# Wider products for the spatial-gate values, the HGRN values and the per-layer gate of a hybrid decoder layer

## The chip, the cores and the metric

The kernel runs on one core of one Trainium2 chip. A core has a matrix engine (TensorE, PE in the profile, with its weight loads as PEld), a vector engine (DVE), a scalar engine (ACT), GpSimd (POOL) and an engine that only issues transfers (SP). The metric is the time of one execution on the device in microseconds; lower is better.

## The reference, cut to what matters

One decoder layer (batch 1, 512 tokens, width 1024, float32) with four token mixers side by side, a gated MLP, a gated per-layer embedding and a final norm. Three products are touched by the change: `v` of the spatial gate, `i` of the HGRN mixer and the gate of the per-layer embedding.

```
proj = rmsnorm(x, norm_mix) @ w_in
xa, xb, xc, xd, g = split(proj)                       # pool, rwkv7, spatial gate, hgrn2, branch gates
u, v = split(gelu(xc))                                # 512 columns each
v = layernorm(v) * ln_w + ln_b;  branch_2 = u * (W_s v + b)
q, f, i = split(xd)                                   # 512 columns each; i: the values of the HGRN recurrence
...
x = x + sum_k(sigmoid(g_k) * (branch_k @ w_branch_k)) @ w_out
x = x + ffn(rmsnorm(x, norm_ffn))
x = x + (p @ ple_proj) * sigmoid(rmsnorm(x, norm_ple) @ ple_gate)      # 1024 columns
out = rmsnorm(x, norm_final)
```

## The kernel before

Every large product is made exactly enough in float32 by splitting both operands into a high and a low part: `mm3` issues three matrix products for each 128 rows of contraction, `hi x hi`, `hi x lo` and `lo x hi` (lines 119, 120 and 121, which is why each large product shows up under these three lines). A weight is loaded by `wload` in chunks of 512 KB on SP's queue, cast to its high part on ACT (line 77) and subtracted to its low part on DVE (line 78). Two buffers hold raw chunks and four each hold high and low parts.

Most products put the weights in the array and move the 512 tokens past them (`gemm`). Three stages want tokens on the partitions, and there `gemm_tok` puts 128 tokens in the array and moves the weight columns past them. For the spatial-gate values (`sg_v`), the HGRN values (`hgrn_v`) and the per-layer gate (`ple`) a weight block (`wcols`) has 256 columns and comes in two chunks of four contraction tiles; each of the four token tiles is taken through all eight contraction tiles, 24 products, into one PSUM buffer, and then evicted, before the next token tile begins. The projection of the embedding at the start (`ple_proj_out`) uses `gemm_tok` with 512 moving columns.

PSUM has two pools of four banks: `mm` (pool `pm`) for the large products, `sm` (pool `ps`) for transposes, norms, the recurrences and the heads. SBUF tiles come from rings; the ring `f` has seven buffers of 512 columns and holds, among others, the four value tiles of the spatial gate, GELU scratch (`gz`) and the branch gates (`gt`).

The work of the mixers is written out in the string `ORDER`. Each word names a part; an exclamation mark makes it urgent, so that the planner puts it ahead of the products that fill in. The planner lays down each engine's instructions in a fixed order when the kernel is built: by priority among those that it holds to be ready, by its own costs. The recurrence of RWKV (`chain.j.half`) issues small products in steps that wait for DVE, and large products stand between the steps. In `ORDER`, `hv.0`, `hv.1` are the two column blocks of `hgrn_v` and `sgv.0`, `sgv.1` those of `sg_v`.

The last stage is the per-layer gate: blocks 0 and 1 run over the four token tiles each; then, for each token tile, blocks 2 and 3 are followed by the final norm of that tile and its stores. The scale `r2` of the norm before the gate is made by `sums` once the first 24 products have been issued.

Of the kernel before, what the change touches and what calls it, by code (L numbers as in the profile page):

```python
# [13 lines left out]
ALU = mybir.AluOpType  # L14
AX = mybir.AxisListType

P = 128
T = 512
NT = T // P
D = 1024  # L20
KD = D // P
# [14 lines left out]
# emission order of the mixers' parts; "!" puts a part before the matrix products that fill in  # L36
# [3 lines left out]
!chain.1.0 !cols hv.1 !sgv.0 !w.3 sgv.1 !chain.1.1 prep.2 !fin.1 merge.0.2 !forms.2 !x.3.1 sgn !sgu.1 sgu.0  # L40
!gate.3.0 merge.2.1 inv.2 !chain.2.0 x.3.0 !merge.2.0 !prep.3 forms.3 !chain.2.1 !gate.3.3 merge.2.2 inv.3
hg.1 !fin.2 merge.2.3 gate.3.2 !hg.0 !chain.3.0 !chain.3.1 fin.3 !out hv.0 !head.0 !head.3 !head.2 ho.3
# [6 lines left out]
def hybrid_kernel(ctx, tc, x, p, norm_mix, w_in, pool_w, pool_scale, rwkv_mu, rwkv_w0, rwkv_w2, rwkv_a0,  # L49
# [25 lines left out]
    # ---------------------------------------------------------------- weights  # L75
# [8 lines left out]
    def rsqrt(r, var, scale, eps, eng=S):  # L84
        """r = (var * scale + eps) ** -0.5 of a few columns."""
        if eng is G:
            V.tensor_scalar(r, var, scale, eps, ALU.mult, ALU.add)
            G.tensor_tensor(r, r, epst[:, 3:4].broadcast_to(list(r.shape)), ALU.pow)
        else:
            S.activation(r, var, AF.Sqrt, scale=scale, bias=epst[:, (NORM_EPS, 64e-5, 1e-5).index(eps):][:, 0:1])  # L90
            V.reciprocal(r, r)
# [6 lines left out]
    def wload(src, a, b, name, early=True):  # L98
        """a k-tiles of b columns as exact sums hi + lo; returns k -> (hi, lo)."""
        g = max(1, 1024 // b)  # L100
        res = []
        with (tc.high_priority() if early else nullcontext()):
            for k0 in range(0, a, g):
                kn = min(g, a - k0)
                raw, hi, lo = (wp.tile([P, 1024], dt, tag=tg, name=f"{tg}_{name}{k0}", bufs=nb)
                               for tg, dt, nb in (("wr", F32, NWR), ("wh", F32R, NWS), ("wl", F32R, NWS)))
                raw, hi, lo = (t[:, :kn * b].rearrange("p (a b) -> p a b", a=kn) for t in (raw, hi, lo))
                nc.sync.dma_start(raw, src[:, k0:k0 + kn, :])
                with (nullcontext() if loaded else tc.high_priority()):
                    split(raw, hi, lo)  # L110
                loaded.append(name)
                res += [(hi[:, k, :], lo[:, k, :]) for k in range(kn)]
        return res

    def wcols(w, c0, name, early=True):
        return wload(w[:, c0:c0 + WB].rearrange("(k p) c -> p k c", p=P), KD, WB, name, early)
# [16 lines left out]
    # -------------------------------------------------------------- constants  # L133
# [27 lines left out]
    # ------------------------------------------------------------------ start  # L161
# [16 lines left out]
    # per-layer embedding's projection, which needs no x; kept in DRAM until the end  # L178
# [49 lines left out]
    def spread(r, name):  # L228
        """r[t] of each token, tokens along the free axis, on every partition."""
        pr = sm_ps(f"ps{name}")  # L230
        for t in range(NT):
            dg = sp.tile([P, P], F32, tag="dg", name=f"dg{name}{t}")
            V.tensor_scalar(dg, ident, r[:, t:t + 1], None, ALU.mult)
            PE.matmul(pr[:, t * P:(t + 1) * P], ones, dg, start=True, stop=True)
        return pr
# [49 lines left out]
    # hgrn lower bound: softmax over the depth axis, inclusive sum less the first  # L285
# [10 lines left out]
    # =============================================================== mixers  # L296
# [3 lines left out]
    def branch_out(k, i, src):  # L300
        """channel tile i of branch k, as hi + lo for the branch's projection."""
        hi = rg.tile([P, T], F32R, tag="bo", name=f"boh{k}_{i}", bufs=NBO)
        lo = rg.tile([P, T], F32R, tag="bo", name=f"bol{k}_{i}", bufs=NBO)
        split(src, hi, lo, V)
        bo.setdefault(k, [None] * 4)[i] = (hi, lo)
# [4 lines left out]
    # ------------------------------------------------------------------ rwkv  # L310
# [8 lines left out]
    # decay and rate weights, hi and lo parts stacked along the contraction: one pass takes both  # L319
# [39 lines left out]
    def c4(t):  # L359
        """a tile as (chunk, head, 64 columns)."""  # L360
        return t.rearrange("p (c h x) -> p c h x", c=HC, h=2)

    def head_sum(o, src, name):
        """sums over each head's channels, on all of them."""
        hi, lo = (rt(f"hs{i}{name}", F32R) for i in range(2))
        split(src, hi, lo, V)
        PE.matmul(o, blkr, hi, start=True, stop=False)
        PE.matmul(o, blkr, lo, start=False, stop=True)
# [24 lines left out]
    def rwkv_prep(j):  # L393
# [20 lines left out]
        # per chunk: decayed -kk to read the state, and decayed r  # L414
# [15 lines left out]
        # columns (B, K) of each chunk's tokens  # L430
# [5 lines left out]
        # the same decayed to the chunk's end  # L436
# [4 lines left out]
        # chunk decays, channels of both heads on the lower partitions  # L441
# [5 lines left out]
        # states (below) and values (above) of both heads  # L447
# [8 lines left out]
        # the second head's reads on the lower partitions; the upper ones take the inverses  # L456
# [5 lines left out]
    def rwkv_forms(j):  # L462
        ard, BK, BD = (rw[j].pop(n) if n != "ard" else rw[j][n] for n in ("ard", "BK", "BD"))
        # rows: tokens of (B, K); columns: their products with A and R (masked)
# [19 lines left out]
        # unit lower triangular inverses of the diagonal 32-blocks, transposed, one block per lane  # L484
# [6 lines left out]
    def rwkv_inverse(j):  # L491
# [20 lines left out]
        # inverses of the 64-blocks from those of the 32-blocks  # L512
# [14 lines left out]
        # the reads of the state take the place of the inverted products  # L527
# [6 lines left out]
    def rwkv_chain(j, half):  # L534
        ard, AR, BKe, M, TA, TT, dec = (rw[j][n] for n in ("ard", "AR", "BKe", "M", "TA", "TT", "dec"))
        # state chain over the chunks
# [41 lines left out]
    def rwkv_finish(j):  # L578
# [3 lines left out]
        # group norm over each head  # L582
# [31 lines left out]
    # ------------------------------------------------------------------ pool  # L614
# [34 lines left out]
    # ------------------------------------------------------------------- sgu  # L649
# [10 lines left out]
    def sg_prep():  # L660
# [8 lines left out]
        # bias over (channel, token): ln_b[c] * rowsum(w)[g, t] + b[g, t], as a product over two rows  # L669
# [16 lines left out]
    def sg_v(vb):  # L686
        vs = sgd["vs"]
        w = wcols(w_in, sg0 + W + vb * WB, f"sgv{vb}")
        for t in range(NT):
            pt = mm_ps(f"psv{vb}_{t}")[:, :WB]  # L690
            gemm_tok(pt, w, hT, t)
            gelu_to(vs[t][:, vb * WB:(vb + 1) * WB], pt, WB, f"v{vb}_{t}")
# [33 lines left out]
    # ------------------------------------------------------------------ hgrn  # L726
# [19 lines left out]
    def hgrn_v(ib):  # L746
        w = wcols(w_in, hc0 + 2 * W + ib * WB, f"hgi{ib}")
        for t in range(NT):
            pt = mm_ps(f"phi{ib}_{t}")[:, :WB]
            gemm_tok(pt, w, hT, t)  # L750
            S.copy(it[t][:, ib * WB:(ib + 1) * WB], pt)
# [110 lines left out]
    # ----------------------------------------------------------------- merge  # L862
# [45 lines left out]
    # ================================================================== ffn  # L908
# [10 lines left out]
    def sums(acc, name):  # L919
        """1 / rms of each token, from squares summed over the channel tiles, tokens on partitions."""  # L920
        pt = sm_ps(f"ps_{name}")
        for t in range(NT):
            PE.matmul(pt[:, 2 * t:2 * t + 2], acc[:, t * P:(t + 1) * P], ones[:, 0:2], start=True, stop=True)
        r = sp.tile([P, NT], F32, tag="rr4", name=f"r_{name}")
        rsqrt(r, pt[:, 0:2 * NT:2], 1.0 / D, NORM_EPS)
        return r
# [104 lines left out]
    # ============================================== per-layer embedding, output  # L1031
# [16 lines left out]
    wpg, r2 = {}, []  # L1048

    def ple(nb, t):  # L1050
        cs = slice((nb % 2) * WB, (nb % 2 + 1) * WB)
        po = mm_ps(f"ppg{nb}_{t}")[:, :WB]
        gemm_tok(po, wpg[nb], x2n, t)
        if not r2:
            r2.append(sums(acc2, "p"))
        sg = bt(f"sg{nb}_{t}")[:, :WB]
        S.activation(sg, po, AF.Sigmoid, scale=r2[0][:, t:t + 1])
        V.tensor_tensor(sg, sg, pp[t, nb // 2][:, cs], ALU.mult)
        xo = x3[t, nb // 2][:, cs]
        V.tensor_tensor(xo, xo, sg, ALU.add)  # L1060
        acc = ssf[:, t, nb:nb + 1]
        if t < NT - 1:
            S.activation(sg, xo, AF.Square, accum_out=acc)
        else:
            V.scalar_tensor_tensor(sg, xo, 1.0, xo, ALU.mult, ALU.mult, accum_out=acc)

    for nb in range(4):
        wpg[nb] = wcols(ple_gate, nb * WB, f"pg{nb}")
        if nb < 2:
            for t in range(NT):  # L1070
                ple(nb, t)
    for t in range(NT):
        ple(2, t)
        if t == NT - 1:
            xn = at("xn", F32)
            G.tensor_tensor(xn, x3[t, 0], nf[0], ALU.mult)
        ple(3, t)
# [40 lines left out]
```

## Time and profile before

| | |
|---|---|
| time, median of 3 runs | 1156.05 us (1155.33 to 1156.17) |
| profiled execution, span from first to last instruction | 1153.9 us |
| profiled execution, own time | not given apart from the span; the median of the runs is 2.15 us above it |
| TensorE busy in the span | 1134.2 us, 98% |
| DVE, ACT, POOL busy | 754.7, 457.0, 205.9 us |
| granted TensorE clock, mean | 0.999 of full |

The profile is of one execution. A product's busy time runs from its start until its result is out, and the next one starts before that; the distance between two starts is what a product takes of the engine. "L119" is line 119 of the kernel; "out<-in" are the program's names. A view says of each instruction or group which engine it is on, its line, its shape and its times; idle time of an engine carries the instruction that ended it.

### The profile page before, as it was taken

The numbers are of one execution on the slowest core, as the hardware profiler recorded it, in microseconds if no ns is written. First come the engines' busy times: TensorE is split into PE (matmuls) and PEld (weight loads), VectorE is DVE, ScalarE is ACT, GpSimd is POOL, SyncE is SP. The second block draws the span as 40 slices with busy tenths as digits, with TensorE's granted clock in tenths as the row PEclk, the third lists the DMA queues.
The fourth block names the chain that finished last, engine by engine and source line by source line (L and its number), as shares of the span: only waits on it lengthen the run. The fifth ranks groups of instructions, "written<-read, shape, count | busy, mean of one in ns | idle before, by whom it ended". The sixth has DMA issues, their size and how long they took to land.

```text
span 1153.9 us, 16004 instructions
## 1 busy us (share of the span) xinstructions
PE 1134.2 (98%) x6170; PEld 919.9 (80%) x6170; DVE 754.7 (65%) x1354; ACT 457.0 (40%) x675; POOL 205.9 (18%) x232
## 2 busy tenths in 40 slices
PE   7999999999999999999999999999999999999997
PEld 5777776887888777878777888888888888888897
DVE  5689986768795688556666565476766766333345
ACT  5733632445342423232122634354444444222262
POOL 8010100001011210101333043223123122110101
PEclk9999999999999999999999999999999999999999
DMA  8433241122323232322111152323323323322522
GB/s 285 140 86 92 79 101 56 53 76 74 105 73 101 74 78 74 101 92 74 55 56 55 56 173 82 109 74 110 95 88 110 93 91 101 101 91 85 171 92 74
DMA packets 121516, 108.92 MB, mean 94 GB/s; under 512 B 17244, under 2 KB 115294, under 8 KB 121440
## 3 DMA queue, kind: packets, MB, share of 16 engines
q1 hardware_dynamic: 102748, 94.74, 26.9%
q10 hardware_dynamic: 17604, 11.02, 3.5%
q0 software_dynamic: 1088, 2.14, 0.6%
q8 instruction: 49, 0.80, 0.3%
q14 instruction: 27, 0.22, 0.1%
HBM read 100.01 MB, written 6.82 MB: 93 GB/s over the span
## 4 chain that ended last, share of the span: by engine, by line
PE 93%; DVE 4%; issue 1%; ACT 1%; DMA 0%; POOL 0%; POOLq 0%; SPq 0%; ACTq 0%; DVEq 0%
PE pgate L121 5%; PE pgate L119 5%; PE pgate L120 5%; PE pfd L119 3%; PE pfv L119 3%; PE pfv L120 3%; PE pfg L119 3%; PE pfg L120 3%; PE pfv L121 3%; PE pfg L121 3%; PE pfd L121 3%; PE pfd L120 3%; PE pbr L119 3%; PE pbr L120 3%; PE pbr L121 2%; PE px L120 2%
## 5 line engine op out<-in xcount | busy, mean ns | idle before, releaser
L121 PE MATMUL pgate<-hT,wl_g 128*128 128x512 f32 x256 | 102.8, 401 | 0.0
L120 PE MATMUL pgate<-hT,wh_g 128*128 128x512 f32 x256 | 102.6, 401 | 0.0
L119 PE MATMUL pgate<-hT,wh_g 128*128 128x512 f32 x256 | 102.3, 399 | 0.0
L119 PE MATMUL pfd<-act_h,wh_fd 128*128 128x512 f32 x176 | 69.3, 394 | 0.0
L121 PE MATMUL pfd<-act_h,wl_fd 128*128 128x512 f32 x176 | 69.0, 392 | 0.0
L121 PE MATMUL pfv<-x1n,wl_fv 128*128 128x512 f32 x176 | 68.6, 390 | 0.0
L119 PE MATMUL pfv<-x1n,wh_fv 128*128 128x512 f32 x176 | 68.6, 390 | 0.0
L120 PE MATMUL pfv<-x1n,wh_fv 128*128 128x512 f32 x176 | 68.6, 390 | 0.0
L120 PE MATMUL pfg<-x1n,wh_fg 128*128 128x512 f32 x176 | 68.5, 389 | 0.0
L121 PE MATMUL pfg<-x1n,wl_fg 128*128 128x512 f32 x176 | 68.5, 389 | 0.0
L119 PE MATMUL pfg<-x1n,wh_fg 128*128 128x512 f32 x176 | 68.5, 389 | 0.0
L120 PE MATMUL pfd<-act_l,wh_fd 128*128 128x512 f32 x176 | 68.3, 388 | 0.0
L78 DVE TENSOR_TENSOR wl_fd<-wr_fd,wh_fd 128x1024 fp32r<-128x1024 f32 (+1 forms) x24 | 29.2, 1216 | 57.0 <-ACT wh_fd L77 57.0
L1012 POOL TENSOR_TENSOR cv<-cv,cg 128x512 f32<-128x512 f32 x22 | 28.4, 1292 | 170.2 <-DVE cv L990 170.2
L121 PEld LDWEIGHTS pgate<-hT,wl_g 128*128 128x128 f32 x256 | 48.1, 188 | 10.3 <-issue 0.9
L120 PEld LDWEIGHTS pgate<-hT,wh_g 128*128 128x128 f32 x256 | 48.1, 188 | 9.7
L119 PEld LDWEIGHTS pgate<-hT,wh_g 128*128 128x128 f32 x256 | 48.1, 188 | 9.6 <-issue 0.2
L77 ACT CAST wh_g<-wr_g 128x1024 fp32r<-128x1024 f32 x32 | 33.3, 1047 | 45.4 <-PE pgate L120 15.0
L119 PE MATMUL pbr<-boh,wh_br 128*128 128x512 f32 x128 | 51.1, 400 | 0.0
L120 PE MATMUL pbr<-bol,wh_br 128*128 128x512 f32 x128 | 51.0, 398 | 0.0
L121 PE MATMUL pbr<-boh,wl_br 128*128 128x512 f32 x128 | 50.6, 395 | 0.0
L78 DVE TENSOR_TENSOR wl_g<-wr_g,wh_g 128x1024 fp32r<-128x1024 f32 x32 | 43.2, 1352 | 8.7 <-ACT wh_g L77 4.6
(455 smaller groups left out, 3008.6 us busy)
## 6 DMA issues: line engine op xcount, KB each, us to landing
wr_g<-in_w_in_dram SPq DMA_DIRECT2D x32, 512.0 KB, 3.6
wr_fg<-in_ffn_up_dram SPq DMA_DIRECT2D x22, 512.0 KB, 3.5
wr_fv<-in_ffn_up_dram SPq DMA_DIRECT2D x22, 512.0 KB, 3.6
wr_fd<-in_ffn_down_dram SPq DMA_DIRECT2D x20, 512.0 KB, 3.4
wr_br<-in_w_branch_dram SPq DMA_DIRECT2D x16, 512.0 KB, 3.5
wr_rkv<-in_w_in_dram SPq DMA_DIRECT2D x12, 512.0 KB, 4.8
wr_wo<-in_w_out_dram SPq DMA_DIRECT2D x8, 512.0 KB, 4.3
wr_pg<-in_ple_gate_dram SPq DMA_DIRECT2D x8, 512.0 KB, 5.5
```

What stands on the lines that cost most here:

```text
L77: S.copy(hi, src)
L78: lo_eng.tensor_tensor(lo, src, hi.bitcast(F32), ALU.subtract)
L119: PE.matmul(o, l[0], r[0], start=first, stop=False)
L120: PE.matmul(o, l[0], r[1], start=False, stop=False)
L121: PE.matmul(o, l[1], r[0], start=False, stop=last)
L1012: G.tensor_tensor(c, c, cg[i], ALU.mult)
```

## The change

`sg_v`, `hgrn_v` and the first half of the per-layer gate take a weight block of 512 columns (`wcols4`, four chunks of two contraction tiles) and move all of them past a token tile in one product. `gemm_tok4` takes a pair of contraction tiles through all four token tiles before it goes to the next pair, so four PSUM buffers are filled side by side. The second half of the per-layer gate (512 columns) goes token tile by token tile into buffers of the `sm` pool; its last token tile is done in two halves of 256 columns. Evictions become 512 wide, apart from that last tile. In `ORDER` the two entries of each values stage become one: `sgv` where `sgv.0` was, `hv` where `hv.0` was. Both weight blocks of the per-layer gate are named ahead of it, and its `sums` comes after the first 96 products. Comment lines are removed as well.

```diff
-!chain.1.0 !cols hv.1 !sgv.0 !w.3 sgv.1 !chain.1.1 prep.2 !fin.1 merge.0.2 !forms.2 !x.3.1 sgn !sgu.1 sgu.0
+!chain.1.0 !cols !sgv !w.3 !chain.1.1 prep.2 !fin.1 merge.0.2 !forms.2 !x.3.1 sgn !sgu.1 sgu.0
...
-hg.1 !fin.2 merge.2.3 gate.3.2 !hg.0 !chain.3.0 !chain.3.1 fin.3 !out hv.0 !head.0 !head.3 !head.2 ho.3
+hg.1 !fin.2 merge.2.3 gate.3.2 !hg.0 !chain.3.0 !chain.3.1 fin.3 !out hv !head.0 !head.3 !head.2 ho.3
...
+    def gemm_tok4(os, w, m):
+        n = len(w)
+        for k0 in range(0, n, 2):
+            for t in range(NT):
+                for k in range(k0, k0 + 2):
+                    mm3(os[t], [h[:, t * P:(t + 1) * P] for h in m[k]], w[k], k == 0, k == n - 1)
+
+    def wcols4(w, c0, name):
+        return wload(w[:, c0:c0 + T].rearrange("(k p) c -> p k c", p=P), KD, T, name)
...
-    def sg_v(vb):
+    def sg_v():
         vs = sgd["vs"]
-        w = wcols(w_in, sg0 + W + vb * WB, f"sgv{vb}")
+        w = wcols4(w_in, sg0 + W, "sgv")
+        pts = [mm_ps(f"psv{t}") for t in range(NT)]
+        gemm_tok4(pts, w, hT)
         for t in range(NT):
-            pt = mm_ps(f"psv{vb}_{t}")[:, :WB]
-            gemm_tok(pt, w, hT, t)
-            gelu_to(vs[t][:, vb * WB:(vb + 1) * WB], pt, WB, f"v{vb}_{t}")
+            gelu_to(vs[t], pts[t], W, f"v{t}")
...
-    def hgrn_v(ib):
-        w = wcols(w_in, hc0 + 2 * W + ib * WB, f"hgi{ib}")
+    def hgrn_v():
+        w = wcols4(w_in, hc0 + 2 * W, "hgi")
+        pts = [mm_ps(f"phi{t}") for t in range(NT)]
+        gemm_tok4(pts, w, hT)
         for t in range(NT):
-            pt = mm_ps(f"phi{ib}_{t}")[:, :WB]
-            gemm_tok(pt, w, hT, t)
-            S.copy(it[t][:, ib * WB:(ib + 1) * WB], pt)
+            S.copy(it[t], pts[t])
...
-    wpg, r2 = {}, []
-
-    def ple(nb, t):
-        cs = slice((nb % 2) * WB, (nb % 2 + 1) * WB)
-        po = mm_ps(f"ppg{nb}_{t}")[:, :WB]
-        gemm_tok(po, wpg[nb], x2n, t)
+    wpg, r2 = [wcols4(ple_gate, n * T, f"pg{n}") for n in range(2)], []
+
+    def ple(n, t, po, c0=0, cn=T):
         if not r2:
             r2.append(sums(acc2, "p"))
...
-    for nb in range(4):
-        wpg[nb] = wcols(ple_gate, nb * WB, f"pg{nb}")
-        if nb < 2:
-            for t in range(NT):
-                ple(nb, t)
+    V.memset(ssf, 0.0)
+    pts = [mm_ps(f"ppg0_{t}") for t in range(NT)]
+    gemm_tok4(pts, wpg[0], x2n)
     for t in range(NT):
-        ple(2, t)
-        if t == NT - 1:
+        ple(0, t, pts[t])
+    for t in range(NT):
+        if t < NT - 1:
+            po = sm_ps(f"ppg1_{t}")
+            gemm_tok(po, wpg[1], x2n, t)
+            ple(1, t, po)
+        else:
             xn = at("xn", F32)
             G.tensor_tensor(xn, x3[t, 0], nf[0], ALU.mult)
-        ple(3, t)
+            for c0 in range(0, T, WB):
+                po = sm_ps(f"ppg1_{t}_{c0}")[:, :WB]
+                gemm_tok(po, [[h[:, c0:c0 + WB] for h in wk] for wk in wpg[1]], x2n, t)
+                ple(1, t, po, c0, WB)
```

## Rows read from the trace of the kernel before

**Rows 1.** The page's head and busy table, whole span (us, share, instructions).

```profile
span 1153.9 us, 16004 instructions
...
PE 1134.2 (98%) x6170; PEld 919.9 (80%) x6170; DVE 754.7 (65%) x1354; ACT 457.0 (40%) x675; POOL 205.9 (18%) x232
```

**Rows 2.** The chain that ended last, by engine.

```profile
PE 93%; DVE 4%; issue 1%; ACT 1%; DMA 0%; POOL 0%; POOLq 0%; SPq 0%; ACTq 0%; DVEq 0%
```

**Rows 3.** Windows: stretch, its length, each engine's busy us, clock, DMA share, GB/s.

```profile
0.00:25.00 25.00, 18.45 (x75) 14.35 (x76) 12.04 (x26) 12.92 (x23) 23.14 (x76) 1.00 0.89 287
...
212.00:262.00 50.00, 50.00 (x449) 45.10 (x448) 35.08 (x96) 23.00 (x46) 0.00 (x0) 1.00 0.25 72
...
532.00:650.00 118.00, 115.80 (x699) 92.29 (x698) 76.92 (x138) 36.63 (x47) 33.82 (x39) 1.00 0.20 63
...
1098.00:1146.00 48.00, 48.00 (x403) 47.93 (x401) 25.89 (x54) 22.95 (x54) 4.45 (x5) 1.00 0.24 78
```

**Rows 4.** Timeline, TensorE, per-layer gate: first and last of 19 products in a row.

```profile
1109.80 0.28 PE L120 MATMUL ppg<-wl_pg,x2n 128*128 128x256 f32 x1
...
1111.96 0.28 PE L120 MATMUL ppg<-wl_pg,x2n 128*128 128x256 f32 x1
```

**Rows 5.** Timeline, TensorE, up-projection: first and last of 15 products in a row.

```profile
799.78 0.39 PE L119 MATMUL pfg<-x1n,wh_fg 128*128 128x512 f32 x1
...
802.95 0.39 PE L121 MATMUL pfg<-x1n,wl_fg 128*128 128x512 f32 x1
```

**Rows 6.** Timeline, TensorE, down-projection: first and last of 10 products in a row.

```profile
1059.71 0.39 PE L119 MATMUL pfd<-act_h,wh_fd 128*128 128x512 f32 x1
...
1061.77 0.39 PE L119 MATMUL pfd<-act_h,wh_fd 128*128 128x512 f32 x1
```

**Rows 7.** Timeline, TensorE, embedding's projection: first and last of 34 products in a row.

```profile
15.15 0.39 PE L120 MATMUL ppp<-wl_plep,pTh 128*128 128x512 f32 x1
...
22.85 0.40 PE L121 MATMUL ppp<-wh_plep,pTl 128*128 128x512 f32 x1
```

**Rows 8.** Tile view: one of three lines each; ns min/median/max, first and last start.

```profile
L119 PE MATMUL psv<-wh_sgv,hT x64: 277/283/386, 221.2 to 261.5; 128*128 128x256 f32 x64
...
L119 PE MATMUL phi<-wh_hgi,hT x64: 278/283/681, 212.1 to 531.9; 128*128 128x256 f32 x64
...
L119 PE MATMUL ppg<-wh_pg,x2n x128: 278/283/365, 1098.6 to 1145.7; 128*128 128x256 f32 x128
```

**Rows 9.** Tile view of the 512-wide GELU's scratch (spatial-gate u).

```profile
L652 ACT ACTIVATE gzu<-psu x4: 583/598/599, 313.0 to 335.5; 128x512 f32<-128x512 f32 x4
L653 DVE SCALAR_TENSOR_TENSOR gzu<-gzu,psu x4: 668/675/687, 313.6 to 336.2; 128x512 f32<-128x512 f32 x4
L654 ACT ACTIVATE gzu<-gzu x4: 622/628/633, 314.3 to 337.2; 128x512 f32<-128x512 f32 x4
L655 DVE TENSOR_TENSOR sgu<-gzu,psu x4: 677/679/689, 315.0 to 338.5; 128x512 f32<-128x512 f32 x4
```

**Rows 10.** Waits: who waited for whom, us in total, times, longest us.

```profile
ACT gt L870 <- POOL merged L888: 19.2, 3, 7.5
```

**Rows 11.** Timeline: the per-layer gate's norm, its first sigmoid, and the last product.

```profile
1101.97 0.95 PE L923 MATMUL ps_p<-ones,acc 128*128 128x2 f32 x8
...
1103.40 0.26 ACT L90 ACTIVATE r_p<-ps_p,epst 128x4 f32<-128x4 f32 x1
...
1105.25 0.47 ACT L1057 ACTIVATE sg<-ppg,r_p 128x256 f32<-128x256 f32 x1
...
1145.92 0.28 PE L121 MATMUL ppg<-wh_pg,x2n 128*128 128x256 f32 x1
```

**Rows 12.** Timeline, ACT: the fourth weight cast of the per-layer gate.

```profile
1094.74 1.05 ACT L77 CAST wh_pg<-wr_pg 128x1024 fp32r<-128x1024 f32 x1 [0.32 <-PE pfd L120]
```

**Rows 13.** Groups of DVE from 1098 us: busy us, mean ns | idle before.

```profile
L1085 DVE SCALAR_TENSOR_TENSOR x<-x,rf,nf 128x512 f32<-128x512 f32 x7 | 5.0, 749 | 2.7 <-POOL rf L88 2.7
L78 DVE TENSOR_TENSOR wl_pg<-wr_pg,wh_pg 128x1024 fp32r<-128x1024 f32 x4 | 4.8, 1223 | 2.8 <-ACT wh_pg L77 2.8
```

More of the change, by code (lines that the diff above doesn't have):

```diff
@@ L1047, in hybrid_kernel @@
     ssf = sp.tile([P, NT, 4], F32, tag="ssf", name="ssf", bufs=1)
-    wpg, r2 = {}, []
-    def ple(nb, t):
-        cs = slice((nb % 2) * WB, (nb % 2 + 1) * WB)
-        po = mm_ps(f"ppg{nb}_{t}")[:, :WB]
-        gemm_tok(po, wpg[nb], x2n, t)
+    wpg, r2 = [wcols4(ple_gate, n * T, f"pg{n}") for n in range(2)], []
+    def ple(n, t, po, c0=0, cn=T):
         if not r2:
             r2.append(sums(acc2, "p"))
-        sg = bt(f"sg{nb}_{t}")[:, :WB]
+        cs = slice(c0, c0 + cn)
+        sg = bt(f"sg{n}_{t}_{c0}")[:, :cn]
         S.activation(sg, po, AF.Sigmoid, scale=r2[0][:, t:t + 1])
-        V.tensor_tensor(sg, sg, pp[t, nb // 2][:, cs], ALU.mult)
-        xo = x3[t, nb // 2][:, cs]
+        V.tensor_tensor(sg, sg, pp[t, n][:, cs], ALU.mult)
+        xo = x3[t, n][:, cs]
         V.tensor_tensor(xo, xo, sg, ALU.add)
-        acc = ssf[:, t, nb:nb + 1]
+        acc = ssf[:, t, 2 * n + c0 // WB:][:, 0:1]
         if t < NT - 1:
```

## Prediction

> **What bounds the kernel now.** I read the page's busy table first: TensorE is busy for 98% of the span and no other engine is over 65% [rows 1]. The chain that ended last agrees: 93% of it is TensorE [rows 2]. A busy TensorE isn't a fast one, since a matrix product's duration overlaps the next one's, so I then read stretches [rows 3] and, inside them, the time from one product's start to the next one's, which is what the engine really pays. Around the spatial-gate values (212 to 262 us) and in the per-layer gate (1098 to 1146 us) TensorE has no idle time at all and the granted clock is 1.00, the 2.4 GHz level; even where the HGRN heads run (532 to 650) it idles only 2.2 of 118 us. So a nanosecond taken off a product's pitch is a nanosecond off the end, as long as the order of work stays as dense as it is.
>
> **What the change removes.** The three stages issue products with 256 moving columns: 192 for the spatial-gate values (64 on each of three lines), as many for the HGRN values, 384 for the per-layer gate [rows 8]. The change turns pairs of them into single ones of 512 columns, except for the last token tile's second half, which keeps 48 narrow ones. So 96 + 96 + 168 = 360 pairs become 360 products, and 360 weight loads go with them.
>
> What a pair costs: in the per-layer gate 18 products start in 1111.96 - 1109.80 = 2.16 us, 120 ns each [rows 4]; a pair is 240 ns. What a wide product costs is shown elsewhere in the same kernel, with three answers. In the up-projection 14 start in 3.17 us, 226.4 ns [rows 5]. In the down-projection 9 start in 2.06 us, 228.9 ns [rows 6]. In the projection of the embedding at the start, the one place where weights already move 512 wide past stationary token tiles, 33 start in 7.70 us, 233.3 ns [rows 7]. A pair thus gives back 240 - 226.4 = 13.6 ns at best and 6.7 ns at worst: over 360 pairs 4.9 or 2.4 us. The last row is nearest in the roles of its operands, but it was taken while the DMA engines were 89% busy, against 24 to 25% in the stages that change [rows 3]; and the narrow pitch, which has the same roles, fits the fastest row: a fixed part f and a part per column give f + 256c = 120 and f + 512c = 226.4, so f = 13.6 ns, c = 0.416 ns. I take the middle row, 229 ns: 11 ns a pair, **4.0 us**: 1.85 in the per-layer gate, 1.06 in each of the other two.
>
> The Trainium skill (TensorE: Matmul & The Clock Gate, Back-to-back issue gap) gives the spacing of bare products at the full clock as columns over 2.4 GHz plus about 2.5 ns. By it a pair gives back only 2.5 ns, an estimate of 0.9 us in all, and halving the count would be worth nothing that can be measured. The trace speaks against that: between 120 and 226.4 ns the fixed part is 13.6 ns [rows 4, 5].
>
> **What it adds.** (1) Four PSUM banks at once. All four `mm` buffers belong to the four token tiles from the first weight chunk to the last. The product can't start a tile before its bank is emptied, and no other wide product can fill in meanwhile; the recurrence's small products, which use the other four banks, still can. At the start, tile t needs its bank 6 x 229 ns = 1.37 us after tile t-1, so only an eviction that is over a microsecond late shows. I charge 0.3 us over the two mixer stages; the bounds are 0 and the rival below. At the end of the product tile 0 finishes 3 x 1.37 = 4.1 us before tile 3, so its eviction runs under the rest.
>
> (2) Evictions of 512 columns in place of 256. GELU takes 598 + 675 + 628 + 679 = 2.58 us for a 512-wide tile [rows 9], off TensorE, and DVE is free for 15 of 50 us there [rows 3]. Two narrow ones need more fixed time than one wide one, so both engines gain slightly; not on the path, 0.
>
> (3) Weight chunks. They stay 512 KB, four for 512 columns as before, cast and split at the same cost. Each is now used for 24 products, 5.5 us, and then let go, where two chunks used to be held for a whole 11.5 us product. The four hi/lo slots hold the whole first block of the per-layer gate: the fourth cast of `wpg` in the run before already starts at 1094.7 [rows 12], before the stage begins. The second block's last chunk waits for the slot that comes free when the first block ends, takes 1.05 us of cast and 1.22 us of DVE [rows 12, 13], and is wanted after the second block's first 18 products, 4.1 us in. It is hidden by 1.8 us; without that cover it would cost the 2.3 us. DMA rows grow from 1 to 2 KB: hidden before and after, 0.
>
> (4) The norm of the per-layer gate, `r2`, is now asked for after all 96 products of the first block, not after the first 24. Before, its sums started at 1101.97 and the first sigmoid at 1105.25, 3.3 us later [rows 11]. Now the block ends near 1098.5 + 96 x 229 ns = 1120.5, and the first sigmoid falls near 1124.5. TensorE doesn't wait, as the second block writes the other four banks. What is late is ACT and DVE: between 1124.5 and the last product near 1143.9 DVE owes seven wide tiles of two 0.68 us operations, one extra square of 0.7, six final scalings of 0.75 [rows 9, 13], and some 2.5 us of small ones and of the last tile's first half: 9.5 + 0.7 + 4.5 + 2.5 = 17.2 us of 19.4. It fits, and I cost it at 0; the cover is 2 us. The last tile stays in two narrow halves, so what follows the last product (it starts at 1145.92 [rows 11], and the span ends at 1153.9: 8.0 us) is unchanged. The memset of `ssf` is off the path.
>
> (5) The order. `hv.1`, 11.5 us of products that filled the waits of the second recurrence, moves to `hv.0`'s place. The spatial-gate product alone (22 us) now fills there, and as much filler is added at the third recurrence and the heads. Filler is moved, not lost; I cost it at 0, but everything between is planned anew, and I allow 1.5 us either way.
>
> **Sum.** -4.0 + 0.3 = -3.7 us. The profiled execution's span is 1153.9 and should become 1150.2; the median of the runs lies 2.15 us above the span, so 1156.05 - 3.7 = **1152.3 us**.
>
> **Rivals.** *The banks bind (slower).* One place: the end of the spatial-gate product. The GELUs need a buffer of the ring `f` (seven), of which `wT`, the bias and the four value tiles hold six. The four GELUs then run one behind the other, 4 x 2.7 = 10.8 us with handovers, starting 4.1 us before the product ends, so the last bank comes free 6.7 us after it. The gate products that follow write those banks, and their sigmoids want the same ring. For it: ACT already waited up to 7.5 us for a gate's buffer, which POOL's merge held [rows 10]. Against it: the next products take 24 x 229 ns = 5.5 us a bank, and the banks come free at -1.4, +1.3, +4.0 and +6.7, each before it is asked for. It decides if DVE serves the first GELU over 1.4 us late and the recurrence has no products ready then. Price: the full 6.7 us, 1156.05 - 4.0 + 6.7 = 1158.8.
>
> *The end piles up (same).* If `r2` comes 2 us later than I count, or DVE takes the work in another order, ACT and DVE still work on old tiles when the last product ends, and the 1.85 us of the last stage are lost: 1156.05 - 4.0 + 0.3 + 1.85 = 1154.2. For it: seven tiles in 19 us instead of spread over 48. Against it: the 2 us of cover.
>
> *The width gives little (same).* A wide product with moving weights costs 233.3 ns, as in the one row of its kind: 1156.05 - 2.4 + 0.3 = 1153.9. Against it: the DMA share of that row, and the fixed part of 13.6 ns. By the Trainium skill's 2.5 ns (the page and section named above) this rival would end at 1155.4, an estimate.
>
> **How the numbers follow.** Chances: the forecast 0.61, the width giving little 0.12, the end piling up 0.12, the banks or the new order costing more than the products give 0.15. A measurement of this kernel can tell 0.2%, 2.3 us, from no change: faster means under 1153.7. The forecast's own bounds are 1156.05 - 4.9 - 1.5 = 1149.6 and 1156.05 - 2.4 + 0.3 + 1.5 = 1155.4. With most of the slow rival below 1158 taken in, the range is **1149.4 to 1158.0**; the forecast alone 1149.6 to 1155.4. Parts of the two middle cases fall just under 1153.7, so faster is 0.66, same 0.19, slower 0.15.
>
> **What would show it.** Right: TensorE's instructions fall by 360; starts of the three stages' wide products lie 226 to 233 ns apart, in the k-pair order; the per-layer gate's products end some 2 us sooner after 1098 than now; 8.0 us still lie between the last product's start and the end. The banks' rival would show as idle time of TensorE, or gaps of over a microsecond between starts, just after the spatial-gate product, with ACT or DVE named as releaser; the pile-up as more than 8.0 us after the last product's start, DVE busy throughout; the narrow gain as starts at 233 ns or more. The prediction is wrong if the mixers' stretch, up to 700 us, changes by more than 4 us either way: then the planned order, not the width, made the time.

## The result and the profile after

The changed kernel is slower: median 1165.96 us (1165.55 to 1166.38) against 1155.69 for the kernel before, ratio 1.0091 with an interval of 1.0079 to 1.0103. The forecast was 1152.3 us.

The page's head and busy table after, to be held against [rows 1]: the span is 10.7 us longer, and TensorE issues 360 products fewer, as counted. It is busy as long as before; the new time is idle time, and products at a lower clock.

```profile
span 1164.6 us, 15211 instructions
...
PE 1134.3 (97%) x5810; PEld 898.7 (77%) x5810; DVE 749.5 (64%) x1331; ACT 448.7 (39%) x641; POOL 207.6 (18%) x232
```

The last stage separates the two places of loss. Timeline of TensorE after, per-layer gate: its first product, the first and last of 53 in a row, its last one.

```profile
1109.17 0.48 PE L119 MATMUL ppg<-wh_pg,x2n 128*128 128x512 f32 x1
...
1116.09 0.39 PE L120 MATMUL ppg<-wl_pg,x2n 128*128 128x512 f32 x1
...
1127.88 0.39 PE L121 MATMUL ppg<-wh_pg,x2n 128*128 128x512 f32 x1
...
1154.36 0.28 PE L121 MATMUL ppg<-wh_pg,x2n 128*128 128x256 f32 x1
```

Here 52 distances take 11.79 us, 226.7 ns each, where a narrow pair took 240 [rows 4]. First to last product takes 45.2 us; before it was 1098.56 to 1145.92, 47.4 [rows 8, 11]. So the width gave 2.2 us, and what follows the last product grew from 8.0 to 1164.6 - 1154.36 = 10.2 us: all of it given back. The gate's first product comes 10.6 us later than before (1098.56 and 1109.17); that loss lies in the mixers.

Windows after (as [rows 3]: PE, PEld, DVE, ACT, POOL busy, clock, DMA share, GB/s), and below them two of before for the stretch in which the loss begins. After, TensorE is busy for 19.67 of the 25 us from 275 on, before for all 25.

```profile
212.00:262.00 50.00, 50.00 (x317) 35.62 (x315) 36.04 (x96) 23.83 (x40) 1.12 (x3) 1.00 0.28 83
275.00:300.00 25.00, 19.67 (x78) 15.75 (x77) 16.32 (x21) 8.66 (x10) 1.86 (x3) 0.88 0.31 90
300.00:325.00 25.00, 23.72 (x140) 19.20 (x139) 17.37 (x37) 7.29 (x14) 2.64 (x2) 0.99 0.16 32
```

```profile
275.00:300.00 25.00, 25.00 (x113) 20.62 (x112) 19.84 (x29) 10.65 (x14) 1.30 (x1) 1.00 0.21 64
300.00:325.00 25.00, 24.25 (x149) 20.06 (x149) 21.63 (x42) 9.71 (x17) 3.56 (x5) 1.00 0.38 101
```

Timeline of TensorE after, at the stall (290 to 301 us). `pk` and `pb` are small products of `prep.2`, the preparation of the third recurrence; between them DVE and ACT work through a chain with two reciprocals.

```profile
286.97 0.40 PE L378 MATMUL pk<-hs0k,blkr 128*128 128x512 f32 x1
287.21 0.39 PE L379 MATMUL pk<-hs1k,blkr 128*128 128x512 f32 x1
...
289.73 0.40 PE L121 MATMUL pbr<-boh,wl_br 128*128 128x512 f32 x1
295.46 0.77 PE L119 MATMUL psu<-hT,wh_sgu 128*128 128x512 f32 x1 [5.33 <-DVE merged L896]
296.02 0.63 PE L120 MATMUL psu<-hT,wh_sgu 128*128 128x512 f32 x1
...
300.29 0.58 PE L121 MATMUL psu<-hT,wl_sgu 128*128 128x512 f32 x1
300.71 0.39 PE L119 MATMUL psu<-hT,wh_sgu 128*128 128x512 f32 x1
...
302.55 0.40 PE L378 MATMUL pb<-hs0b,blkr 128*128 128x512 f32 x1
```

The same two products before:

```profile
273.87 0.50 PE L367 MATMUL pk<-hs0k,blkr 128*128 128x512 f32 x1
...
300.06 0.40 PE L367 MATMUL pb<-hs0b,blkr 128*128 128x512 f32 x1
```

Before, 26.2 us lie between the first `pk` and the first `pb` product, and the trace has 114 products in them, 25.7 us by their pitches. After, 15.6 us lie between, with 31 products: 7.1 us. The chain itself takes 15.3 to 16.6 us where too little stands beside it (after, e2 to e4, e9, e11, e12 and e15); what is missing is the products. DVE shows the inside of the stall, timeline after:

```profile
288.02 1.23 DVE L78 TENSOR_TENSOR wl_g<-wr_g,wh_g 128x1024 fp32r<-128x1024 f32 x1 [1.49 <-ACT wh_g L77]
289.17 0.42 DVE L418 TENSOR_SCALAR nr<-nr 128x512 f32<-128x512 f32 x1
289.62 3.35 DVE L419 RECIPROCAL nr<-nr 128x512 f32<-128x512 f32 x1
292.89 1.16 DVE L78 TENSOR_TENSOR wl_g<-wr_g,wh_g 128x1024 fp32r<-128x1024 f32 x1
293.97 0.74 DVE L420 SCALAR_TENSOR_TENSOR kk<-xb,cols_b,nr 128x512 f32<-128x512 f32 x1
294.63 0.68 DVE L896 TENSOR_TENSOR merged<-gt,pbr 128x512 f32<-128x512 f32 x1
```

The branch product `pbr` was finished just after 289.73, but its eviction (L896) stands on DVE behind the reciprocal, a weight split and `kk`. It releases the `mm` bank that TensorE waits for and the ring buffer that ACT waits for. Then comes a second loss: from 296.02 to 300.29 ten distances take 4.27 us, 427 ns each, with a granted clock of 0.88 in the row for 275 to 300 us; from 300.71 the starts are 230 ns apart again. Twelve products (295.46 to 300.71) at some 0.2 us extra each are 2.4 us. The Trainium skill (TensorE: Matmul & The Clock Gate, Wait — 56ns, not 53.3ns?) gives 426.7 ns from start to start for 512 columns on the lower level, 1.2 GHz; this trace agrees.

Where the 12.7 us went that the mixers lost (10.6, and the 2.1 that the prediction had them gain): 15.6 - 7.1 = 8.5 us around this chain against 26.2 - 25.7 = 0.5 before, so 8.0 here. About 1.1 us are a wait at 362 us that before doesn't have. The HGRN heads, from their first `phl` product to their last `pho`, take 116.2 us (545.66 to 661.84) against 114.2 (536.97 to 651.13): 2.0. The rest, about 1.6 us, is spread.

### The profile page after: what moved, and what is told of

It is laid out like the page before. It is cut to its first block, busy times and chain, and to the rows that moved or that the text cites. A ratio compares the mean times of both kernels' runs of the same rounds, so it can differ in the third digit from the quotient of the medians.

```text
span 1164.6 us, 15211 instructions
## 1 busy us (share of the span) xinstructions
PE 1134.3 (97%) x5810; PEld 898.7 (77%) x5810; DVE 749.5 (64%) x1331; ACT 448.7 (39%) x641; POOL 207.6 (18%) x232
## 5 line engine op out<-in xcount | busy, mean ns | idle before, releaser
L78 DVE TENSOR_TENSOR wl_g<-wr_g,wh_g 128x1024 fp32r<-128x1024 f32 x32 | 41.0, 1283 | 10.7 <-ACT wh_g L77 10.4
```

Source lines behind the costliest of these rows:

```text
L78: lo_eng.tensor_tensor(lo, src, hi.bitcast(F32), ALU.subtract)
```

## The experiments

Medians of each run and of the kernel before on the same chip, and the ratio with its interval. SG: spatial-gate values; HV: HGRN values; gate: per-layer gate.

| run | what | us | before | ratio |
|---|---|---|---|---|
| e1 | only the gate wide | 1155.37 | 1155.35 | 0.9997 [0.9988, 1.0007] |
| e2 | only SG wide (urgent), HV as before | 1165.14 | 1155.35 | 1.0081 [1.0065, 1.0098] |
| e3 | only HV wide, at its late place | 1166.92 | 1155.35 | 1.0098 [1.0083, 1.0113] |
| e4 | nothing wide, `hv.1` moved | 1168.15 | 1155.35 | 1.0109 [1.0093, 1.0124] |
| e5 | changed kernel, `hv` early | 1172.86 | 1155.53 | 1.0145 [1.0128, 1.0162] |
| e6 | changed kernel, ring `f` of 8 | 1166.21 | 1155.53 | 1.0088 [1.0066, 1.0110] |
| e7 | e1, norm early | 1154.65 | 1155.53 | 0.9991 [0.9982, 1.0000] |
| e8 | e1, stores on SP | 1154.42 | 1155.53 | 0.9987 [0.9978, 0.9997] |
| e9 | changed kernel, `prep.2` urgent | 1166.04 | 1154.98 | 1.0097 [1.0082, 1.0112] |
| e10 | changed kernel, `x.3.1`, `sgu.1` not urgent | 1160.41 | 1154.98 | 1.0050 [1.0035, 1.0065] |
| e11 | e9, norm early, stores on SP | 1165.70 | 1154.98 | 1.0094 [1.0077, 1.0111] |
| e12 | e4, `prep.2` urgent | 1171.69 | 1154.98 | 1.0147 [1.0132, 1.0162] |
| e13 | only SG wide, not urgent | 1161.54 | 1155.47 | 1.0052 [1.0038, 1.0066] |
| e14 | e13 and e16 | 1160.75 | 1155.47 | 1.0042 [1.0029, 1.0054] |
| e15 | before, `!sgv.1` | 1166.89 | 1155.47 | 1.0098 [1.0084, 1.0112] |
| e16 | e1, norm early, stores on SP | 1154.15 | 1155.47 | 0.9985 [0.9976, 0.9994] |
| e17 | SG wide, one bank at a time, not urgent | 1155.04 | 1155.59 | 0.9996 [0.9987, 1.0005] |
| e18 | e17 and e16 | 1153.85 | 1155.59 | 1.0002 [0.9977, 1.0027] |

**One part alone (e1 to e4).** Each of e1 to e3 takes the changed code of one stage and leaves the others, with their words in `ORDER`, as before; e4 has no wide product.

```diff
 e2  !chain.1.0 !cols hv.1 !sgv !w.3 !chain.1.1 ...
 e3  !chain.1.0 !cols !sgv.0 !w.3 sgv.1 !chain.1.1 ...   !out hv !head.0
 e4  !chain.1.0 !cols !sgv.0 !w.3 sgv.1 !chain.1.1 ...   !out hv.0 hv.1 !head.0
```

> Only the per-layer gate is wide; the mixers and their order are those of before. Theory 1 (the products save, the end gives it back): 168 wide products at 227 ns replace 336 at 120 ns, about 2 us less of TensorE, but the scaling and the stores of the first token tiles come late and hold the sigmoids on ACT, so the time from the last product's start to the end grows from 8.0 us to about 10: no change, 1155 to 1156.5 us. Rival (the predicted sum): the end stays 8.0 us after the last product's start and the time falls by 1.9 us, to about 1153.8.

> Only the spatial-gate values are wide, as one entry in the order; the HGRN values stay narrow, hv.1 in its early place. Theory 1 (filler moved): the stall near 290 us comes from hv.1 leaving, so there is none here: 1154 to 1156 us. Theory 2 (four banks and wide GELUs change the plan): the stall of 5 us and the half clock after it show here: 1163 to 1166 us.

> Only the HGRN values are wide, as one entry in the late place; the spatial-gate values and the per-layer gate are as before. Theory 1 (filler moved): the stall near 290 us shows here, 1163 to 1166 us. Theory 2 (four banks of the spatial gate): no stall, 1154 to 1156 us.

> No product is wide; hv.1 alone is moved from its early place to stand behind hv.0. Theory 1 (filler moved): the stall near 290 us shows although no product changed, 1164 to 1167 us, a little above the kernel with the wide HGRN values. Theory 2 (four banks, wide products): the time of before, 1155 to 1157 us.

e1 came out by its first theory: it loses nothing in the mixers and gains nothing in the end. e2 came out against its first theory, since the stall shows with `hv.1` in its early place; e3 and e4 came out by theirs, 0.9 and 1.2 us above the times named. e2, e3 and e4 each lose 10 to 13 us, and each has the stall of the changed kernel: 5.49 us between two starts beyond the product's pitch, in e2 at 302.0, in e3 at 289.7, in e4 at 290.3. In all three, as in the changed kernel, 31 products (11 `pbr`, 20 `psu`) stand between `pk` and `pb`. e4 has no wide product at all, so width isn't needed for the loss.

**Mending the stall from its sides (e5, e6, e9 to e12).** Order edits against the changed kernel, e12 against e4; e6 sets `NF` from 7 to 8; e11 adds to e9 the two edits of e7 and e8 below.

```diff
 e5   -!cols !sgv          +!cols hv !sgv          (and hv out of its late place)
 e9   -!chain.1.1 prep.2   +!chain.1.1 !prep.2     (e12 the same)
 e10  -!x.3.1 sgn !sgu.1   +x.3.1 sgn sgu.1
```

> The whole change, but the one wide hv entry stands where hv.1 stood, so 22 us of products that fill in stay between the start of the second recurrence and merge.0.2. Theory 1 (too little filler lets the merge of the pool branch run into the 3.4 us reciprocal of prep.2): no wait of over 2 us near 290 to 305 us, and the time is that of before less the 2 us of the two wide mixer products: 1152.5 to 1154.5 us. Theory 2 (the four banks and the wide spatial gate make the stall in any order): 1163 to 1166 us.

> The whole change with eight buffers in the ring f instead of seven; the order string is the changed one. Theory 1 (the ring: the first GELU of u waits for the gate buffer that the merge holds, and its PSUM bank with it): the wait near 290 us goes or falls under 2 us, and the half clock behind it with it: 1154 to 1157 us. Rival (DVE alone is late, whatever the ring holds): the wait of 5 us stays, 1163 to 1166 us.

> The whole change with one mark more in the order: prep.2 is urgent, as prep.0, prep.1 and prep.3 are. In the changed kernel its first product pk stands behind 38 products of the urgent sgu.1, and only 31 products (7 us) stand between pk and pb, for a chain over DVE and ACT of 15 us; in the kernel before 26 us of products stand there. With the mark pk moves to the end of the recurrence. Theory 1 (prep.2 was put off by the planner): no wait over 1.5 us from 275 to 325 us, no half clock there, 9 us won: 1155.5 to 1158 us. Rival (whatever the order, the filler that was moved away is missing in this stretch): the waits come back at pb or pg, 1161 to 1166 us.

> The whole change, but the two urgent parts that overtake prep.2, x.3.1 and sgu.1, lose their mark. Theory 1 (they overtake prep.2): pk stands at the recurrence's end again and the wait near 290 us goes, 1155.5 to 1159 us. Rival (missing filler): 1161 to 1166 us.

> The whole change with prep.2 urgent, the per-layer gate's norm after its first 24 products, and all stores of the output on SP. Theory 1 (the products do save 4 us, and two separate places of the order gave it back): stall gone and 8.0 to 8.5 us from the last product's start to the end, 1151.5 to 1154 us. Rival (what is won at one place is lost in the heads or elsewhere): 1155 us or more.

> No product is wide; hv.1 stands behind hv.0, as in the run of the order alone (1168), and prep.2 is urgent. Theory 1: the stall goes although hv.1 stays away, 1156 to 1159 us. Rival (hv.1's filler is needed where it stood): 1163 to 1168 us.

None gets back to the kernel before, and no first theory met its time; e9 and e11 came out by their rivals, e5 and e12 above both times named, e10 between them, and e6 lost most of the wait and kept the time. e5 gives filler to the second recurrence and takes it from the heads: four waits of 1.2 to 1.5 us between 554 and 565, clock 0.73 in 550 to 575. It also has two waits, of 1.26 us before 280.95 and 2.21 us before 288.90, that end when DVE has emptied a bank of the spatial-gate product (L666), the place that the prediction's rival of the banks named. e6 frees ACT, and the wait near 290 shrinks, but the chain behind `pk` hasn't become shorter (17.7 us from `pk` to `pb`); TensorE waits for it later, with a clock of 0.80 in 300 to 325. Timeline of TensorE in e6:

```profile
291.72 0.47 PE L119 MATMUL psu<-hT,wh_sgu 128*128 128x512 f32 x1 [0.98 <-DVE merged L896]
305.24 0.51 PE L378 MATMUL pb<-hs0b,blkr 128*128 128x512 f32 x1 [2.36 <-ACT hs0b L77]
311.44 1.16 PE L484 MATMUL pg<-ard,BK 64*128 64x128 f32 x16 [1.71 <-DVE BK L446]
```

So the full ring is where the lack shows, not its root. e9 puts `pk` ahead of the `psu` products (some 14.7 us of products in a gap of 16.6), and pays at the next chain: 2.20 us before `pg` at 295.76, and 2.28 us before 360.25. e11 has its end mended (last product to end 8.3 us) and the same stalls in the mixers. e12, the same mark without any wide product, is 3.5 us slower than e4. e10 does best of the changed kernels; it has no stall near 290 and one of 3.1 us at 354, where ACT's weight cast stands behind a transfer issue that waits for DVE.

**Mark and width apart (e13 to e15).** e13 is wide and keeps the order of before; e15 is the kernel before with one character more.

```diff
 e13  !chain.1.0 !cols hv.1 sgv !w.3 !chain.1.1 ...
 e15  !chain.1.0 !cols hv.1 !sgv.0 !w.3 !sgv.1 !chain.1.1 ...
```

> Only the spatial-gate values are wide (one product, four banks); its entry loses its urgent mark, and the HGRN values stay two narrow blocks at their old places, so that the planner's order from the second recurrence on is that of before. Filler theory (the loss comes from products taken away from the waits of the second recurrence and its successor, not from width or banks): no idle time of TensorE over 3 us between 270 and 320 us, granted clock 0.99 or more there, time 0.5 to 2 us under the kernel before. Rival (four banks at once and the 512-wide GELUs bind): an idle stretch of 4 to 6 us near 290 to 305 us and 8 to 10 us more than before.

> Spatial-gate values wide and not urgent, HGRN values as before, per-layer gate wide with its norm after 24 products and all its stores on SP's queue. Filler theory: both gains show, some 1 us from the spatial gate and 1.3 us or more from the per-layer gate: 2 to 3.5 us under the kernel before. Rival (the saved products are given back wherever an engine behind them is late): within 1 us of the kernel before.

> The kernel before with one exclamation mark more, on the second block of the spatial-gate values; nothing is wide, nothing else moves. Filler theory: the second block no longer stands in the waits of the second recurrence, so the stall comes as in the changed kernel: 4 to 6 us of TensorE idle near 290 us, the granted clock low behind it, 8 to 12 us more than before. Rival (it takes the width, the banks or the HGRN block's move): within 1.5 us of the kernel before.

e15 came out by its filler theory: the mark alone is enough for the stall. Its TensorE timeline has the same picture, 13 us later:

```profile
300.18 0.39 PE L379 MATMUL pk<-hs1k,blkr 128*128 128x512 f32 x1
...
308.42 0.76 PE L119 MATMUL psu<-hT,wh_sgu 128*128 128x512 f32 x1 [5.32 <-DVE merged L896]
...
315.50 0.40 PE L378 MATMUL pb<-hs0b,blkr 128*128 128x512 f32 x1
```

Between `pk` and `pb` are again 31 products, and 11 us are lost with no wide product in the kernel. In the trace of before, 79 narrow `psv` products stand between the first and the last step of the second recurrence (239.4 to 275.0 us). In e15 (249.2 to 286.0) and in the changed kernel (236.6 to 274.2) none does, and `pgate`, `pbr` and `px` products stand there, the ones that otherwise stand beside `prep.2`. Tile views, one of three lines each, of the changed kernel and of e15: their `psv` products are over before these steps begin.

```profile
L119 PE MATMUL psv<-wh_sgv,hT x32: 389/389/747, 206.9 to 233.6; 128*128 128x512 f32 x32
```

```profile
L119 PE MATMUL psv<-wh_sgv,hT x64: 279/283/283, 221.0 to 245.8; 128*128 128x256 f32 x64
```

The traces of e2, e3 and e4 have no `psv` product between these steps either: without `hv.1` ahead of it, even the unmarked `sgv.1` of e3 and e4 is over by 235 us. So the mark and the move of `hv.1` take away the same filler, and their losses don't add: the changed kernel, which has both, loses 10.3 us, e15 11.4 and e4 12.8.

e13 met neither of its theories: it is 6.1 us over before. With 121 products behind `pk` the stall near 290 is gone, and another one is there. Timeline of TensorE in e13, then of DVE:

```profile
281.98 0.40 PE L121 MATMUL pbr<-boh,wl_br 128*128 128x512 f32 x1
286.08 0.80 PE L119 MATMUL pbr<-boh,wh_br 128*128 128x512 f32 x1 [3.69 <-DVE sgv L666]
```

```profile
271.34 0.67 DVE L666 TENSOR_TENSOR sgv<-gzv,psv 128x512 f32<-128x512 f32 x1
...
274.20 3.32 DVE L419 RECIPROCAL nr<-nr 128x512 f32<-128x512 f32 x1
...
278.09 0.63 DVE L666 TENSOR_TENSOR sgv<-gzv,psv 128x512 f32<-128x512 f32 x1
...
285.35 0.67 DVE L666 TENSOR_TENSOR sgv<-gzv,psv 128x512 f32<-128x512 f32 x1
```

The GELUs' last steps, which empty the four banks, come one behind the other, with the reciprocal and other work between them; the last bank is let go at 286. That is the rival that the prediction called *The banks bind*, at the end of the spatial-gate product, where this product is the filler. e14 adds the mended gate (below) and is 0.8 us under e13, but 5.3 over before, which neither of its theories had.

**One bank at a time (e17, e18).**

```diff
-        pts = [mm_ps(f"psv{t}") for t in range(NT)]
-        gemm_tok4(pts, w, hT)
         for t in range(NT):
-            gelu_to(vs[t], pts[t], W, f"v{t}")
+            pt = mm_ps(f"psv{t}")
+            gemm_tok(pt, w, hT, t)
+            gelu_to(vs[t], pt, W, f"v{t}")
```

> As e13 (spatial-gate values alone wide, not urgent), but token tile by token tile into one bank at a time: 24 products of 512 columns, then the tile's GELU, as before the change; all four weight chunks are held to the end. Bank theory (e13's 3.9 us near 282 us came from four banks that wait for four GELUs together): no idle stretch over 1.5 us near 280 us, and 4 to 6 us under e13, 0 to 1.5 us under the kernel before. Rival (any spatial-gate product that stands in the second recurrence as one part collides with the inverse's DVE chain, or the held weight chunks make the next weights late): an idle stretch of 2 us or more between 255 and 290 us, and 3 us or more over the kernel before.

> e17 and e16 in one kernel: spatial-gate values wide, one bank at a time, not urgent; per-layer gate wide with the early norm and all stores on SP's queue; HGRN values as before. If both theories hold the gains add: 1.5 to 3.5 us under the kernel before. If e17's rival holds: 1 us or more over it.

Past the kernel's start no two starts in e17 lie more than 1.0 us beyond the pitch, and it is 6.5 us under e13 (1161.54 - 1155.04): the four banks cost that. Some 5.5 us of it are the wait and the slower products behind it (in e13 eight distances from 281.98 to 289.37 take 7.4 us, 1.8 by the pitch). The window of 275 to 300 us is that of before again:

```profile
275.00:300.00 25.00, 25.00 (x114) 20.34 (x112) 19.82 (x29) 8.34 (x12) 1.61 (x3) 1.00 0.22 65
```

The theory of the banks named 4 to 6 us under e13. The last product of e17 starts at 1145.30, 0.6 us sooner than before; the interval for the time reaches over 1, so a gain of e17 over before isn't shown. e18 has a median 1.7 us under before, and ten of its twelve runs lie at 1152.65 to 1154.89; two others, at 1166.5 and 1167.3, make its interval wide, and its gain isn't shown either.

**The end (e7, e8, e16).** All on e1. The norm early means that the first 24 products of `gemm_tok4`, two of the eight contraction tiles for all token tiles, are followed by `sums`; the stores of the second column half go to SP's queue instead of ACT's.

```diff
-    gemm_tok4(pts, wpg[0], x2n)
+    gemm_tok4(pts, wpg[0][:2], x2n[:2], last=False)
+    r2.append(sums(acc2, "p"))
+    gemm_tok4(pts, wpg[0][2:], x2n[2:], first=False)
...
-            (nc.sync, nc.scalar)[n].dma_start(out2[t * P:(t + 1) * P, n * T:(n + 1) * T], x3[t, n])
+            nc.sync.dma_start(out2[t * P:(t + 1) * P, n * T:(n + 1) * T], x3[t, n])
```

> Only the per-layer gate is wide, as in the run of that part alone, but its norm r2 is asked for after the first 24 products, not after 96. Theory 1 (the late norm piles the sigmoids, products and squares of the first block onto the end): the distance from the last product's start to the end falls from 10.3 to 8.0 to 8.5 us, 1153.0 to 1153.9 us. Rival (the wide evictions themselves are too slow for the end): it stays near 10 us, 1155 to 1156 us.

> Only the per-layer gate is wide, the norm late as in the change, but all stores of the output are issued by SP; before, ACT issues half of them and its next sigmoid stands behind a store that waits for DVE's scaling. Theory 1 (ACT's queue is what delays the end): the third tile's sigmoid starts when its product ends, 2 us sooner, and the end follows the last product's start by about 8.5 us: 1153.3 to 1154 us. Rival (DVE's own pile is the cause, ACT only shares it): 1 us or less is won, 1154.3 to 1155.4 us.

> Per-layer gate alone wide, its norm after 24 products and all its stores on SP's queue; the mixers are those of before. If the late norm and ACT's waiting store issue together hold the end: the last product's start lies 8.0 to 8.5 us before the span's end, and the time is 1.3 to 2.3 us under before. Rival (DVE's own work after the last products holds it): 9 us or more between the two, and under 1.2 us gained.

First to last product of the gate, and last product to the end of the span, from the timelines:

| | before | after | e1 | e7 | e8 | e16 | e18 |
|---|---|---|---|---|---|---|---|
| gate's products, us | 47.4 | 45.2 | 45.2 | 45.2 | 45.2 | 45.2 | 45.2 |
| last product to end, us | 7.98 | 10.24 | 10.25 | 9.41 | 9.02 | 8.26 | 8.31 |

The late norm accounts for 0.8, the stores for 1.2, both for 2.0 of the 2.3 us. So e7 fell between its two theories, e8 came out by its rival's time, and e16 met its first theory. In the changed kernel this chain shows on ACT. Timeline of all engines after: the norm and the first sigmoid, then two store issues of ACT, while DVE still scales what is to be stored, and the sigmoids behind.

```profile
1131.51 0.95 PE L934 MATMUL ps_p<-ones,acc 128*128 128x2 f32 x8
...
1134.11 0.26 ACT L90 ACTIVATE r_p<-ps_p,epst 128x4 f32<-128x4 f32 x1
...
1135.96 1.27 ACT L1066 ACTIVATE sg<-ppg,r_p 128x512 f32<-128x512 f32 x2
...
1148.23 2.69 ACTq L1101 DMA_DIRECT2D out_dram<-x  x2
...
1149.12 1.42 DVE L1100 SCALAR_TENSOR_TENSOR x<-x,rf,nf 128x512 f32<-128x512 f32 x2 [0.67 <-POOL rf L88]
1151.02 0.69 ACT L1066 ACTIVATE sg<-ppg,r_p 128x512 f32<-128x512 f32 x1 [4.23 <-DVE x L1100]
...
1157.02 0.47 ACT L1066 ACTIVATE sg<-ppg,r_p 128x256 f32<-128x256 f32 x1 [2.73 <-DVE x L1069]
```

The last half sigmoid starts 2.7 us after the last product. In e16 it starts right behind it:

```profile
1144.75 0.47 ACT L1064 ACTIVATE sg<-ppg,r_p 128x256 f32<-128x256 f32 x1 [2.34 <-PE ppg L121]
```

e16 beats both kernels: 1154.15 us, 1.3 us under before, with an interval that stays under 1 (0.9976 to 0.9994).

## Why the prediction was wrong, point by point

- **What bounds it, and the width.** Right: 360 products fewer, at a pitch of 226.7 ns in the gate, against the 229 that I took. The gate's products take 2.2 us less (1.85 predicted). For the spatial gate one profiled execution of e17 is 0.6 us sooner where 1.06 was predicted; the ratio doesn't show it. The HGRN values were never wide without a move in the order, so their share is not shown alone.
- **(5) The order: this step failed.** It said "Filler is moved, not lost; I cost it at 0" with 1.5 us either way, which rests on no row, and "The spatial-gate product alone (22 us) now fills there". The diff itself contradicts the second sentence: `sgv.1` had no exclamation mark and `!sgv` has one. The product became urgent as a whole, ran from 206.9 to 234.0 us instead of 221 to 261 [rows 8], and nothing of it was left for the second recurrence. Its steps took `pgate`, `pbr` and `px` products instead, and `prep.2`'s 15 us chain stood beside 7.1 us of products instead of 25.7. e15 (the mark alone) and e4 (the move of `hv.1` alone) each give this stall, and 11.4 and 12.8 us. The amount of filler was the same; its place is what paid, and moving it was not to be costed at 0.
- **(1), and the rival of the banks.** Not in the changed kernel: after the spatial-gate product TensorE is busy for all of 212 to 262 us, since the product runs early and its banks aren't wanted. But the mechanism is real: with the filler kept in place, e13 shows it, and against e17 it costs 6.5 us, where the rival's price was 6.7. That the two figures lie so close is in part luck: the price was for the wait alone, and in e13 the slower products behind a wait of 3.7 us are in the 6.5 as well. The chance for slower rested mostly on this place, and the time was lost elsewhere.
- **(2) and (3)** held: no row shows TensorE waiting for a weight chunk in the changed stages, and DVE and ACT are busy 5.2 and 8.3 us less than before in the span.
- **(4) The end: this step failed too.** "It fits, and I cost it at 0; the cover is 2 us", and what follows the last product "is unchanged". The first sigmoid came 26.8 us after the gate's first product (26.0 estimated), so the lateness of the norm was sized rightly. What I left out is that ACT also issues stores, and that such an issue waits on DVE's scaling: the sum of 17.2 us in 19.4 was DVE's alone, and ACT does no sigmoid during the 2.69 us of two store issues. The rival *The end piles up* describes it, with 1.85 us where 2.3 were lost.
- Its test "the mixers' stretch, up to 700 us, changes by more than 4 us" was the right one to name: it was 10.6 us by the gate's start.

What stays open: whether HGRN values 512 wide can pay, since one product has one place and the two blocks filled two; and what the changed kernel would do with the mark alone taken off, which no run shows.

## What to carry to other kernels

When a diff joins two entries of a hand-written order, check which priority each half had and what stood beside each of the long chains behind it: for each chain, add up the products between the one that starts it and the one that needs it, and compare with its length. A saving per instruction counts only if the stages behind it can take the faster pace: here three further edits (banks one at a time, the norm early, the stores off the engine with work to do) decided whether 13 ns a pair reached the end. An eviction that stands behind a long operation in a fixed engine order holds its PSUM bank as surely as a slow engine does.

## What the runs showed of the hardware that was not expected

A stall cost more than its length: after 5.33 us of idle time ten products in a row started 427 ns apart instead of 227 to 230 (the lower of the two clock levels, 1.2 GHz), and the twelve products up to 300.71 cost 2.4 us on top. After 3.69 us in e13 the starts from 287.30 to 289.00 us lie 425 ns apart in the same way. e10 had an idle stretch of 3.1 us at 354 us with a granted clock of 1.00 in the row for 350 to 375 us, and e6 had waits of 2.36 and 1.71 us and a clock of 0.80 in the row for 300 to 325 us; so in these rows the length of a single wait doesn't tell by itself whether the clock falls.

A reciprocal of a 128x512 tile took 3.35 us on DVE, five times the 0.68 us of the two-operand operation of L896 on a tile of that size.
